# A two-layer attention and ConvFFN trunk on one Trainium2 core: near-attention operands and results through DRAM scratch, earlier sums of h, and two more gate pairs a layer as seven-product blocks

## The chip, the core and the metric

The kernel runs on one core of one Trainium2 chip. The metric is the device time of one execution in microseconds (us). The kernel before takes 2670.75 us, the median of three runs (2669.71 to 2671.51). The engines are TensorE (PE; its weight loads have a row of their own, PEld), VectorE (DVE), ScalarE (ACT) and GpSimd (POOL). SyncE (SP) issues nearly all DMAs. Each engine takes its instructions in order.

## The reference

Sequence length and model width are 1024, there are 2 layers, all data are fp32. One layer computes:

```
h = rmsnorm(x, norm1)
qa, ka, va, qb, kb, vb, gate_pre = split(h @ w_in)
o_a = dilated_mixture(qa, ka, va)        # 12 heads of 64: 3 groups of 4 heads,
                                         # (window, dilation) = (128, 1), (512, 4), (2048, 16)
o_b = stick_breaking_attention(qb, kb, vb)             # 4 heads
g_a, g_b = split(sigmoid(gate_pre + b_gate))           # 1024 columns each
x = x + (g_a * (o_a @ w_br[:256]) + g_b * (o_b @ w_br[256:])) @ w_o
up = rmsnorm(x, norm2) @ w_up            # 2816 columns of a, 2816 of v
x = x + (gelu(causal_conv(a)) * v) @ w_down
```

In `dilated_mixture` each query sees 128 earlier keys at its group's step; the three groups' results are mixed by their softmax denominators. Group 0 (dilation 1) is the undilated branch, called near below; groups 1 and 2 are far. Stick-breaking attention is causal, with a cumulative product along the keys.

## The kernel before

**Numbers in two parts.** Every matmul operand is split into a high part `hi` (rounded, by ACT) and a rest `lo` (by DVE, `split`, L135 and L140). A product is three matmuls: hi by hi, hi by lo, lo by hi. The tokens are two halves `n` of 512, the width 8 chunks of 128; `H[n]` holds h in its two parts.

**Plain product** (`product`, L171 to L173): one unit of 128 columns of `w_in` against both halves takes 2 x 8 x 3 = 48 matmuls of 512 columns. `gate` (L1145, tile `g_ps`), `keys`, `queries` use it.

**Pair in seven products** (`pair`, `seven`, L935 to L937, tiles `i_a`, `i_b`, `i_c`): two units of 128 columns against both halves are a 2 x 2 block product done with seven block products instead of eight: 7 x 4 x 3 = 84 matmuls. For this it needs four sums of blocks of h: S1 = b12 - b11, S2 = b22 - S1, S3 = b22 - b12, S4 = b21 - S2 (`block_sums`, tile `h_sum`), where b11, b12, b21, b22 are halves of `H[1]`, `H[0]` in their first and last four chunks. S1 to S3 take two buffers each of the six of tag `e8`; S4 is written over b12 and thus needs every plain product done.

**The attentions and their filler.** `attend` walks through the items by hand: 16 stick-breaking items (B00 to B17), then near items (N), then 16 far items (T). An item is scores on PE, then softmax or scan work on DVE and ACT, then for each set of key blocks `turn` (transposes on PE, split by ACT and DVE) and `apply` (matmuls with V). After each such slot `dense.advance(rate)` adds `rate` steps of dense work; a step is 6 matmuls of 512 columns (12 of 256 for `values`). `RATE_B` has the rates of the B items, `RATE[1]` that of N, `RATE[2:]` those of T. The class `Dense` takes units from `main`, then `plain` (gates, `PLAIN` of them), then `seven` (the remaining gates as pairs). Units of `main` marked True are pairs and start once `plain` is empty. `dense.side` holds the steps of the sums, one popped at each `advance`.

**Near operands.** `keys` and `queries` keep k and q of one pair of heads in `e8` tiles `kt`, `qt` and in `ql` (tag `ql`, two buffers); per half four or two 64-row ACT copies and two 64-row DVE operations. A near item is one head (N00 to N11), with four scores and five turns, at rate 0.85. Results go to tile `on` (tag `xa`, four buffers) and for stick-breaking to `ob` (one `e8` buffer), which goes to DRAM once.

**Far operands.** `pair_kq` and `pair_v` store to DRAM (`tk`, `tv`) and each far item loads its own; item T00 may start when both v pairs, the first two kq pairs and near item N11 are done, plus `LEAD` = 6 steps. The other two kq pairs and the four gate pairs run beside the far items or after them (`finish`).

**FFN.** The first two of 22 units run in plain products while `norm` for the second half is still being made (L492 to L495), the others in seven products (`up`); `up` has a POOL subtraction at L1514. The buffers of tag `pt` (six) hold most short-lived 128 x 512 tiles.

PE's order is the program's. On the other engines and on SP the scheduler orders by priority; `tc.high_priority` moves instructions ahead.

Of the kernel before, what the change touches and what calls it, by code (L numbers as in the profile page):

```python
# [16 lines left out]
P = 128  # L17
# [25 lines left out]
RATE = (0.68, 0.85, 0.72, 0.62)  # L43
RATE_B = (0.9, 1.6, 0.75, 1.1, 0.65, 0.9, 0.6, 0.3)
PLAIN = 8
# [12 lines left out]
def trunk_kernel(ctx, tc, x, norm1, w_in, b_gate, w_br, w_o, norm2, w_up, conv_w, conv_b, w_down, norm_f, out, depth=None, probe=None):  # L58
# [58 lines left out]
    dn = [dr.tile([4, T], F32, name=f"dn{i}") for i in range(2)]  # L117

# [92 lines left out]
    class Dense:  # L211
# [4 lines left out]
        def __init__(self):  # L216
            self.main, self.plain, self.seven, self.done = [], [], [], set()
            self.side, self.later, self.hooks = [], {}, []
            self.now = self.nxt = None
            self.due, self.count = 0.0, 0  # L220
            self.started = False
            self.scored = self.applied = self.kq = self.v = 0
# [46 lines left out]
        def step(self):  # L269
            while True:  # L270
                if self.now is None:
# [4 lines left out]
                    if self.now[2] and not self.started:  # L276
# [4 lines left out]
                        self.started = True  # L281
                if self.nxt is None:
# [44 lines left out]
    def attend(dense, items):  # L327
# [4 lines left out]
        for i, (name, first, rest, rate, make) in enumerate(items):  # L332
# [37 lines left out]
            for j, f in enumerate(seq):  # L370
                if nxt and j >= at:
# [100 lines left out]
    def norm(n, gain, tag, then=None, keep=False):  # L472
# [17 lines left out]
        for e in range(KD):  # L490
            hf = kept_f32(n, e) if keep else small("hf")
            dve.scalar_tensor_tensor(hf, xc(n, e), gain[:, e : e + 1], rb, ALU.mult, ALU.mult)  # L492
            hi, lo = H[n][0][:, e, :], H[n][1][:, e, :]
            act.copy(hi, hf)
            (pool if e % 2 and not (keep and n) else dve).tensor_tensor(lo, hf, f32(hi), ALU.subtract)  # L495
# [80 lines left out]

    def head(l):
# [51 lines left out]
    def stick_item(pr, s, qp):  # L629
        if "ob" not in R:  # L630
            R["ob"] = big("ob")
        q, k, vt, ob = R["qb", pr], R["kb", pr], R["vb"], R["ob"]
# [52 lines left out]
        def apply(kb):  # L685
# [24 lines left out]
    def near_item(pr, s):  # L710
        if s == 0:
            R["st0", pr] = sb.tile([P, 2, 2, 8], F32, tag="st0", bufs=2, name="st0")
        if "on" not in R:
            R["on"] = sb.tile([P, 2, T], F32, tag="xa", bufs=4, name="on")
        q, k, vt, on, st = R["q0", pr], R["k0", pr], R["v0"], R["on"], R["st0", pr]
        slot = 2 * pr + s
        got, shared = {}, {}

        def score(m):
            if m == 0:  # L720
                shared["bias"] = sb.tile([P, 512], F32, tag="bias", name="bias0")
                dve.tensor_scalar(shared["bias"][:, 0:256], base0, SLOPES[slot], None, ALU.mult)
            if m % 2 == 0:
                got[m // 2] = sb.tile([P, T], F32, tag="p4", bufs=4, name="p0")
            z = bank("s", "z0")
            todo = []
            for j in range(2):
# [3 lines left out]
                scores(zz, *(t[:, s, b * P : b * P + P] for t in q), k[:, s, (b - 1) * P + c : b * P + P])  # L731
                todo.append((b, c, zz))
            for b, c, zz in todo:
                pp = got[b // 4][:, 256 * (b % 4) + c : 256 * (b % 4) + 256]
                nm = st[:, 0, s, b : b + 1]
                dve.tensor_tensor_reduce(pp, zz, shared["bias"][:, c:256], 1.0, 3e38, ALU.add, ALU.min, nm)
                act.activation(pp, pp, AF.Exp, bias=nm, scale=-1.0, accum_out=st[:, 1, s, b : b + 1])

        def turn(i, some):
            tp = bank("t", "t0")  # L740
            w = 0
            for kb, bs in some:
                for b in bs:
                    col = 256 * (b % 4) + (P if b == kb else 0)
                    pe.transpose(tp[:, w * P : (w + 1) * P], got[b // 4][:, col : col + P], ident)
                    w += 1
            shared[i] = parts(tp, w * P, "p0")

        def apply(i, some, n, first, last):
# [4 lines left out]
            for kb, bs in some:  # L754
                c0, nb = (bs[0] - 4 * n) * P, len(bs) * P
                for p in (0, 1):
# [3 lines left out]
                        shared[i][p][:, w * P : w * P + nb],  # L760
# [5 lines left out]
            if last:  # L766
                fold(on[64 * s : 64 * s + 64, pr, n * HF : (n + 1) * HF], o)
# [8 lines left out]
        micro = []  # L776
        for n, sets in enumerate(
            (
                [[(0, [0, 1]), (1, [1, 2])], [(2, [2, 3]), (3, [3])]],
                [[(3, [4]), (4, [4, 5])], [(5, [5, 6]), (6, [6, 7])], [(7, [7])]],  # L780
            )
        ):
            for i, some in enumerate(sets):
                micro.append(
                    (
                        lambda i=(n, i), some=some: turn(i, some),
                        lambda i=(n, i), some=some, n=n, f=(i == 0), la=(i == len(sets) - 1): apply(i, some, n, f, la),
                    )
                )
        return [lambda m=m: score(m) for m in range(4)], micro  # L790


# [14 lines left out]
    def far_item(dense, pr, s, r, share):  # L807
        i = 8 * pr + 4 * s + r
        slot = 2 * pr + s
        if s == 0 and r == 0:  # L810
            R["st1", pr] = sb.tile([P, 2, 2, 2, 4], F32, tag="st1", bufs=2, name="st1")
            R["ot", pr] = None
        st = R["st1", pr]
# [127 lines left out]
    def block_sums():  # L941
# [4 lines left out]
        def first(t, a, b, i):  # L946
            if i == 0:
                if "r" not in keep:
                    keep["r"] = quarter("h_sum")
                new_s(t)  # L950
            r, (ah, al), (bh, bl) = keep["r"][:, i, :], a()[i], b()[i]
            one = pool.tensor_tensor(r, f32(al), f32(bl), ALU.subtract)
            if "last" in keep:
                tc.add_manual_dep(one.ins, keep["last"], NO_SYNC, reason="one sum after the other")
            pool.tensor_tensor(r, r, f32(ah), ALU.add)
# [1063 lines left out]
```

## Time and profile before

| | |
|---|---|
| median of 3 runs | 2670.75 us |
| profiled execution, its own time | 2670.63 us |
| span in that profile | 2668.9 us |
| ACT busy | 1350.2 us (51%) |
| instructions | 36664 |

The profile gives busy time by engine, by stage (a window of the span) and by group of instructions. A matmul's duration is the time it is in the array, and several are in it at once: matmuls of 512 columns that last 389 ns each start much closer together than that. So the sum of their durations is more than the time they take, and a busy PE may still be held up by a fraction between starts. The rate has to be read from counts over a window, or from starts in the timeline.

### The profile page before, as it was taken

To read this page: it belongs to the slowest core of one execution; us is meant where nothing else is said; L and a number is where in the kernel's file an instruction comes from. 1 tells how busy PE (TensorE), PEld (TensorE's weight loads), DVE (VectorE), ACT (ScalarE), POOL (GpSimd) and SP (SyncE) were. 2 spreads that over 40 slices of the span, in tenths; PEclk is the share of its full clock that TensorE was granted. 3 is DMA by queue.
4 is the path that set the end of the run, shared out by engine and by line. 5 is a ranking of instruction groups with operands and counts; after the bars stand their busy time and mean duration, and the time that the engine had idled before them with its cause. 6 is when DMAs were issued, how large, how long until landed. Compare 5 with 4: busy or idle time off the path is not lost.

```text
span 2668.9 us, 36664 instructions
## 1 busy us (share of the span) xinstructions
PE 2651.1 (99%) x13084; PEld 2227.4 (83%) x13084; DVE 2030.3 (76%) x3087; ACT 1350.2 (51%) x2490; POOL 648.9 (24%) x473
## 2 busy tenths in 40 slices
PE   9999999999999999999999999999999999999999
PEld 8988888878888888888889888888888888888888
DVE  5877856685888888897658777566858888898865
ACT  6556645564545554432445565455645454554225
POOL 2003210121233443321210051110321343343200
PEclk9999999999999999999999999999999999999999
DMA  5212178573244544688411122885632544446863
GB/s 183 64 52 83 58 206 242 187 260 99 80 145 139 174 139 158 228 313 321 152 40 40 51 81 84 220 246 182 233 94 68 180 144 149 151 166 246 339 243 118
DMA packets 360194, 424.19 MB, mean 159 GB/s; under 512 B 20692, under 2 KB 289356, under 8 KB 357964
## 3 DMA queue, kind: packets, MB, share of 16 engines
q1 hardware_dynamic: 359996, 421.85, 47.6%
q8 instruction: 103, 1.69, 0.3%
q14 instruction: 79, 0.65, 0.1%
q10 hardware_dynamic: 16, 0.00, 0.0%
HBM read 278.07 MB, written 143.72 MB: 158 GB/s over the span
## 4 chain that ended last, share of the span: by engine, by line
PE 90%; DVE 7%; issue 1%; ACT 1%; DMA 1%; POOL 0%; DVEq 0%; ACTq 0%; SPq 0%; POOLq 0%
PE u_a L935 5%; PE u_a L936 5%; PE u_a L937 5%; PE d_ps L1647 5%; PE d_ps L1648 5%; PE d_ps L1649 5%; PE u_c L935 3%; PE u_c L936 3%; PE u_c L937 3%; PE i_a L935 3%; PE i_a L936 2%; PE i_a L937 2%; PE o_ps L171 2%; PE o_ps L173 2%; PE o_ps L172 2%; PE g_ps L171 2%
## 5 line engine op out<-in xcount | busy, mean ns | idle before, releaser
L140 DVE TENSOR_TENSOR w_lo<-up_a,w_hi 128x512 fp32r<-128x512 f32 x240 | 236.8, 993 | 20.3 <-ACT w_hi L135 20.3
L135 ACT CAST w_hi<-up_a 128x512 fp32r<-128x512 f32 x240 | 149.4, 623 | 183.9 <-PE u_a L936 45.8
L1655 DVE TENSOR_TENSOR x<-x,d_ps 128x512 f32<-128x512 f32 (+1 forms) x228 | 152.0, 672 | 77.9 <-PE d_ps L1649 76.4
L1386 POOL TENSOR_TENSOR cv<-cv 128x512 f32<-128x512 f32 x88 | 131.8, 1508 | 249.3 <-DVE cv L1381 139.4
L140 DVE TENSOR_TENSOR g<-cv,g 128x512 fp32r<-128x512 f32 x154 | 151.2, 983 | 5.2 <-ACT g L135 2.8
L140 DVE TENSOR_TENSOR w_lo<-w_raw,w_hi 128x512 fp32r<-128x512 f32 x144 | 109.4, 762 | 52.8 <-ACT w_hi L135 52.6
L135 ACT CAST w_hi<-w_raw 128x512 fp32r<-128x512 f32 x144 | 89.5, 621 | 111.1 <-PE o_ps L172 64.3
L140 DVE TENSOR_TENSOR w_lo<-in_a,w_hi 128x512 fp32r<-128x512 f32 x120 | 88.9, 740 | 60.4 <-ACT w_hi L135 54.7
L135 ACT CAST w_hi<-in_a 128x512 fp32r<-128x512 f32 x120 | 74.6, 622 | 118.3 <-PE i_c L936 51.3
L1647 PE MATMUL d_ps<-gd_in,w_hi 128*128 128x512 f32 (+1 forms) x340 | 130.3, 383 | 1.6 <-issue 0.7
L1649 PE MATMUL d_ps<-gd_in,w_lo 128*128 128x512 f32 (+1 forms) x340 | 129.8, 382 | 0.0
L1648 PE MATMUL d_ps<-gd_in,w_hi 128*128 128x512 f32 (+1 forms) x340 | 129.8, 382 | 0.0
L935 PE MATMUL u_a<-hh,w_hi 128*128 128x512 f32 x320 | 124.7, 390 | 0.5 <-DVE u L1537 0.5
L937 PE MATMUL u_a<-hh,w_lo 128*128 128x512 f32 x320 | 124.5, 389 | 0.0
L935 PE MATMUL u_a<-t_hi,w_hi 128*128 128x512 f32 x320 | 124.5, 389 | 0.0
L936 PE MATMUL u_a<-hl,w_hi 128*128 128x512 f32 x320 | 124.5, 389 | 0.0
L936 PE MATMUL u_a<-t_lo,w_hi 128*128 128x512 f32 x320 | 124.5, 389 | 0.0
L937 PE MATMUL u_a<-t_hi,w_lo 128*128 128x512 f32 x320 | 124.5, 389 | 0.0
L135 ACT CAST g<-cv 128x512 fp32r<-128x512 f32 x154 | 94.9, 616 | 42.2 <-POOL cv L1386 29.5
L665 DVE TENSOR_TENSOR_SCAN stay<-stay,zero 128x512 f32<-128x512 f32 (+2 forms) x96 | 93.5, 974 | 28.0 <-ACT stay L651 27.4
L1647 PE MATMUL d_ps<-gd_in,wd 128*128 128x512 f32 (+1 forms) x292 | 113.9, 390 | 0.0
L1649 PE MATMUL d_ps<-gd_in,wd 128*128 128x512 f32 (+1 forms) x292 | 112.8, 386 | 0.0
(412 smaller groups left out, 8603.5 us busy)
## 6 DMA issues: line engine op xcount, KB each, us to landing
gd<-g SPq DMA_DIRECT2D x154, 512.0 KB, 3.5
gd_in<-gd SPq DMA_DIRECT2D x154, 512.0 KB, 6.0
up_a<-in_w_up_dram SPq DMA_DIRECT2D x80, 512.0 KB, 5.3
t_kq<-tk SPq DMA_DIRECT2D x32, 768.0 KB, 4.4
wd_raw<-in_w_down_dram SPq DMA_DIRECT2D x22, 1024.0 KB, 12.1
w_raw<-in_w_in_dram SPq DMA_DIRECT2D x80, 256.0 KB, 3.0
in_a<-in_w_in_dram SPq DMA_DIRECT2D x40, 512.0 KB, 3.9
gin<-gs SPq DMA_DIRECT2D x32, 512.0 KB, 4.4
```

The costliest lines, as they stand in the source:

```text
L135: one = act.copy(hi, src)
L140: two = dve.tensor_tensor(lo, src, f32(hi), ALU.subtract)
L171: pe.matmul(o, lh, rh, start=(first and i == 0), stop=False, skip_group_check=share)
L665: one = dve.tensor_tensor_scan(rev, rev, zero[:, 0:1].to_broadcast([P, c1 - c0]), 1.0 if c1 == L else sv[:, c1 : c1 + 1], ALU.mult, ALU.add)
L935: pe.matmul(o, w[0][:, c], rh, start=(first and i == 0), stop=False, skip_group_check=True)
L936: pe.matmul(o, w[0][:, c], rl, start=False, stop=False, skip_group_check=True)
L937: pe.matmul(o, w[1][:, c], rh, start=False, stop=(last and i == 3), skip_group_check=True)
L1386: return lambda: pool.tensor_tensor(dst, a, b, ALU.subtract)
L1647: pe.matmul(o[:, sub], wh[:, c], gh[:, sub], start=(i == 0 and k in (0, 4, 5)), stop=False, skip_group_check=True)
L1648: pe.matmul(o[:, sub], wh[:, c], gl[:, sub], start=False, stop=False, skip_group_check=True)
L1649: pe.matmul(o[:, sub], wl[:, c], gh[:, sub], start=False, stop=(i == m - 1), skip_group_check=True)
L1655: dve.tensor_tensor(x, x, o[:, sub], ALU.add)
```

## The change

- `PLAIN` 8 to 4: four gate units a layer leave the plain products, and two more gate pairs are done in seven products.
- Near k and q: `near_kq` makes the product, splits it over 128 rows with one ACT and one DVE instruction a half, and stores the parts to DRAM (`nk`). Each near item (now half a head, N0 to N7) loads its operands with two DMAs into a buffer of tag `xa`; the load is issued two items ahead, and the item may start 6 steps after (8 for the first, which also waits for the last B item).
- Results: `ob` and `on` pieces are folded into `pt` tiles and stored at once; `on` is loaded back when the far items begin. The `e8` buffer of `ob` is gone.
- Sums: S3 starts when B07 is scored, S1 and S2 when B17 is; S2 = S3 + b11. POOL does 33 of the 48 additions a layer (24 of 40 before), DVE 15. S4 is made in the first six steps of the first pair. Far pairs may start after B17 and beside the near items, no longer after the last near score.
- Rates: B items 0.9 of before; near 0.85 to 1.0; far 0.72 and 0.62 to 0.9 and 0.75. T00 waits 10 steps after its loads, no longer 6.
- FFN: for the second half the last chunk of h has high priority; in `up` the subtraction L1514 goes to DVE for the third unit alone.

```diff
-RATE = (0.68, 0.85, 0.72, 0.62)
-RATE_B = (0.9, 1.6, 0.75, 1.1, 0.65, 0.9, 0.6, 0.3)
-PLAIN = 8
+RATE = (0.68, 1.0, 0.9, 0.75)
+RATE_B = (0.81, 1.44, 0.675, 0.99, 0.585, 0.81, 0.54, 0.27)
+PLAIN = 4
+SUMS = ((1, 0, 0, 0, 0, 6), (1, 1, 0, 1, 2, 8), (1, 2, 0, 2, 4, 10), (1, 3, 0, 0, 7, 12), (2, 0, 1, 3, 9, 11), (2, 1, 0, 1, 9, 14), (2, 2, 1, 3, 11, 13), (2, 3, 1, 3, 13, 15))
...
-                return i < 16 and {"N11", f"1{i // 8}", f"2{i // 8}", "v1", "v2"} <= self.done
+                return i < 16 and {"N7", f"1{i // 8}", f"2{i // 8}", "v1", "v2"} <= self.done
+            while self.near < min(8, self.nscored + 2) and {"B17", f"0{self.near // 4}"} <= self.done:
+                fetch_near(self.near)
+                self.at(LEAD if self.near else 8, lambda i=self.near: self.done.add(f"G{i}"))
+                self.near += 1
...
-                self.at(LEAD, lambda i=self.kq: self.done.add(f"F{i}"))
+                self.at(LEAD if self.kq else 10, lambda i=self.kq: self.done.add(f"F{i}"))
...
+                        for k, f in enumerate(self.first):
+                            self.at(1 + k, f)
...
+            with tc.high_priority(offset=AHEAD) if keep and n and e >= 7 else nullcontext():
...
+    def near_kq(pr, l, off, query):
+        w = weights(w_in[l][:, off : off + P], P)
+        yield
+        for n in range(2):
+            o = bank("ps", "q_ps" if query else "k_ps")
+            yield from product(o, [(w[k], h_part(n, k)) for k in range(KD)])
+            hi, lo = small("nk_h", F32R), small("nk_l", F32R)
+            if query:
+                act.mul(hi, o, -SCALE)
+                dve.scalar_tensor_tensor(lo, o, -SCALE, f32(hi), ALU.mult, ALU.subtract)
+            else:
+                act.copy(hi, o)
+                dve.tensor_tensor(lo, o, f32(hi), ALU.subtract)
+            for s in range(2):
+                rows = slice(64 * s, 64 * s + 64)
+                for src, kind, up in ((hi, 1, 0), (hi, 1, 64), (lo, 2, 0)) if query else ((hi, 0, 0), (lo, 0, 64)):
+                    nc.sync.dma_start(nk[pr][s, up : up + 64, kind, n * HF : (n + 1) * HF], f32(src[rows]))
+            yield
...
-                fold(ob[64 * s : 64 * s + 64, pr, qp * 256 : (qp + 1) * 256], o)
-                if (pr, s, qp) == (1, 1, 3):
-                    nc.sync.dma_start(obd, ob)
+                part = small("ob_p")[64 * s : 64 * s + 64, 0:256]
+                fold(part, o)
+                nc.sync.dma_start(obd[64 * s : 64 * s + 64, pr, qp * 256 : (qp + 1) * 256], part)
...
+    def fetch_near(i):
+        pr, s, n = i // 4, i // 2 % 2, i % 2
+        t = R["nk", i] = sb.tile([P, 2048], F32R, tag="xa", bufs=4, name="n_kq")
+        k0 = 3 * P * n
+        nc.sync.dma_start(f32(t[:, 0 : (n + 1) * HF - k0]), nk[pr][s, :, 0, k0 : (n + 1) * HF])
+        nc.sync.dma_start(f32(t[:, 640:1664]).rearrange("p (a c) -> p a c", a=2), nk[pr][s, :, 1:3, n * HF : (n + 1) * HF])
...
-                fold(on[64 * s : 64 * s + 64, pr, n * HF : (n + 1) * HF], o)
+                part = small("on_p")[64 * s : 64 * s + 64]
+                fold(part, o)
+                nc.sync.dma_start(ond[64 * s : 64 * s + 64, pr, n * HF : (n + 1) * HF], part)
...
+            less = ALU.add if t == 2 else ALU.subtract
+            one = eng.tensor_tensor(r, f32(al), f32(bl), less)
+            eng.tensor_tensor(r, r, f32(ah), ALU.add)
+            one = eng.tensor_tensor(r, r, f32(bh), less)
...
-        series({"B17"}, 3, lambda i: first(3, b22, b12, i), 6, 4)
-        series({"N01s"}, 1, lambda i: first(1, b12, b11, i), 6, 4)
-        for i in range(4):
-            todo.append(({"N01s"}, lambda i=i: less(b22, i)))
-        series({"N11s"}, 2, lambda i: i or new_s(2), 0, 1)
-        series({"plain"}, 4, lambda i: further(4, b21, i), 1, 1)
+        todo += series("B07s", *((3, i, pool, i % 2, 4 * i, 4 * i + 6) for i in range(4)))
+        todo += series("B17s", *((t, i, (pool, dve)[e], slot, at, then) for t, i, e, slot, at, then in SUMS))
+        dense.first = [f for _, f in series("", *((4, i, (pool, dve)[e], slot, at, then) for i, e, slot, at, then in ((0, 0, 0, 0, 4), (1, 1, 3, 0, 2), (2, 0, 1, 2, 6), (3, 1, 3, 3, 5))))]
...
-            *kq("0", 0, {"B07s"}, 0, -SCALE),
-            *kq("0", 1, {"B17s"}, P, -SCALE),
-            (None, {"N11s"}, pair_v(dense, l, 1), True),
+            *kq("0", 0, set(), 0, -SCALE),
+            *kq("0", 1, set(), P, -SCALE),
+            (None, {"B17"}, pair_v(dense, l, 1), True),
...
-            pool.tensor_tensor(a11, a12, a11, ALU.subtract)
+            (dve if j == 2 else pool).tensor_tensor(a11, a12, a11, ALU.subtract)
```

More of the change, by code (lines that the diff above doesn't have):

```diff
@@ L370, in attend @@
             for j, f in enumerate(seq):
+                if pending and name[0] == "N":
+                    begin()
+                    at = max(at, j)
                 if nxt and j >= at:
@@ L491, in norm @@
             hf = kept_f32(n, e) if keep else small("hf")
[L492 to L495, printed above, removed]
+            with tc.high_priority(offset=AHEAD) if keep and n and e >= 7 else nullcontext():
+                dve.scalar_tensor_tensor(hf, xc(n, e), gain[:, e : e + 1], rb, ALU.mult, ALU.mult)
+                hi, lo = H[n][0][:, e, :], H[n][1][:, e, :]
+                act.copy(hi, hf)
+                (pool if e % 2 and not (keep and n) else dve).tensor_tensor(lo, hf, f32(hi), ALU.subtract)
             if e < KD - 1:
@@ L969, in in_two @@
         def in_two(t, i):
-            split(*S[t][i], keep["r"][:, i, :], "waits")
+            split(*S[t][i], keep.pop((t, i)), "waits")
         b11, b12, b21, b22 = (lambda n=n, k=k: half(n, k) for k in range(2) for n in (1, 0))
         todo = []
-        def series(after, t, f, lag, gap):
-            at = {}
-            for i in range(4):
-                at.setdefault(i * gap, []).append(lambda i=i: f(i))
-                at.setdefault(i * gap + lag, []).append(lambda i=i: in_two(t, i))
-            for k in range(3 * gap + lag + 1):
-                todo.append((after, lambda fs=at.get(k, ()): [g() for g in fs]))
@@ L1185, in mixer @@
         dense.seven = [pair_gate(dense, l, e) for e in range(PLAIN // 2, KD)]
-        dense.side = [({"B02"}, zeros)] * (l == 0) + block_sums()
+        dense.side = [({"B02"}, zeros)] * (l == 0) + block_sums(dense)
         def kq(name, pr, after, off, scale):
-            offk, offq = (OFF_KB, OFF_QB) if name == "b" else (OFF_KA, OFF_QA)
+            if name == "0":
+                return [(None, after, near_kq(pr, l, OFF_KA + off, False), False), ("0" + str(pr), after, near_kq(pr, l, OFF_QA + off, True), False)]
+            offk, offq = OFF_KB, OFF_QB
             return [
```

133 lines of the change are left out of this document (72 added, 61 removed).

## The prediction

> **What bounds the kernel now.** I read the page first: engine shares and granted clock.
>
> ```profile
> span 2668.9 us, 36664 instructions
> ...
> PE 2651.1 (99%) x13084; PEld 2227.4 (83%) x13084; DVE 2030.3 (76%) x3087; ACT 1350.2 (51%) x2490; POOL 648.9 (24%) x473
> ...
> PEclk9999999999999999999999999999999999999999
> ```
>
> PE is never idle and its clock never drops, so time goes only where matmuls go, if the busy figure can be trusted. To see how many a busy PE does, I took stages of layer 0 (PE, PEld, DVE, ACT, POOL busy, instructions in brackets): stick-breaking items, near items, four pairs alone, far items, branch products, FFN opening, steady FFN.
>
> ```profile
> 67.00:247.00 180.00, 179.73 (x1058) 157.14 (x1057) 140.40 (x250) 108.29 (x235) 10.94 (x10) 1.00 0.21 59
> 247.00:325.00 78.00, 78.00 (x426) 66.24 (x425) 58.83 (x122) 49.95 (x118) 31.64 (x23) 1.00 0.24 75
> 325.00:410.00 85.00, 84.97 (x391) 69.81 (x390) 49.54 (x75) 36.50 (x64) 10.98 (x8) 1.00 0.70 193
> 410.00:547.00 137.00, 135.61 (x761) 115.31 (x760) 92.27 (x199) 74.39 (x166) 16.36 (x15) 1.00 0.69 215
> 547.00:600.00 53.00, 51.13 (x239) 41.48 (x237) 48.27 (x67) 35.74 (x60) 15.86 (x12) 1.00 0.79 271
> 700.00:760.00 60.00, 59.08 (x263) 48.20 (x263) 53.81 (x87) 32.56 (x55) 9.88 (x8) 1.00 0.28 91
> 760.00:1300.00 540.00, 539.26 (x2376) 445.67 (x2376) 455.75 (x554) 237.92 (x376) 178.93 (x120) 1.00 0.58 206
> ```
>
> In the steady FFN 540 us hold 2376 matmuls: 227 ns each. The timeline there shows the same, beside a duration of 0.39:
>
> ```profile
> 1000.21 0.39 PE L936 MATMUL u_c<-hl,w_hi 128*128 128x512 f32 x1
> 1000.43 0.39 PE L937 MATMUL u_c<-hh,w_lo 128*128 128x512 f32 x1
> 1000.66 0.39 PE L935 MATMUL u_c<-hh,w_hi 128*128 128x512 f32 x1
> ```
>
> So a 512-column matmul is worth **227 ns, not the 390 of its row**, and a step of dense filler (6 of them) 1.36 us. PE's waits that show at all are small and scattered:
>
> ```profile
> PE o L858 <- DVE p1l L140: 2.1, 6, 0.7
> PE br_ps L171 <- DVE gin L1301: 2.0, 4, 0.8
> ...
> PE z L608 <- DVE st L840: 1.5, 3, 0.6
> PE u_ps L172 <- DVE hl L495: 1.3, 2, 0.7
> ```
>
> Each is PE behind DVE. The kernel is bound by matmul count; the next limit is DVE, above all where a stage needs it for 85% or more.
>
> **Part 1, the gates: fewer matmuls.**
>
> ```profile
> L171 PE MATMUL g_ps<-hh,w_hi 128*128 128x512 f32 x256 | 105.6, 412 | 0.0
> L935 PE MATMUL i_b<-hh,w_hi 128*128 128x512 f32 x80 | 33.0, 412 | 0.0
> ```
>
> The 256 are one of three lines of 16 plain gates: 48 matmuls a gate. The 80 are four of the 12 matmuls of one product in each of 20 pairs: 84 a pair. A layer loses four gates (192) and gains two pairs (168): 24 fewer, 48 in both layers. 48 x 0.227 = **-10.9 us**. From the durations (390) it would be -18.7; I take the count, since starts and not ends decide when the next one goes. No other edit adds or removes a PE instruction: the near items keep their scores, transposes and applies, only cut in two.
>
> **Part 2, near operands and results through scratch.** Per layer eight halves of k or q are split on 128 rows instead of 64: ACT goes from 24 operations to 8, DVE from 16 to 8.
>
> ```profile
> L548 ACT ACTIVATE qt<-q_ps 64x512 fp32r<-64x512 f32 x32 | 19.0, 593 | 20.3 <-PE q_ps L173 20.0
> ...
> L559 POOL MEMSET ql<- 64x1024 f32 x16 | 15.2, 949 | 355.2 <-PE z L609 253.4 <-issue 83.0 <-PE nrm_t L478 10.1
> ```
>
> That spares ACT some 9 us a layer and POOL four memsets (3.8 us), all off the path. SP gets 40 stores of k and q, 16 loads, 15 more stores of `ob`, 8 of `on` and one load: 80 more per layer, and four once for zeros. The nearest rows, by issue time (min, median, max) and by KB and landing:
>
> ```profile
> L1146 SPq DMA_DIRECT2D gs<-gt x32: 319/338/343, 132.8 to 1635.7; - x32
> L1092 SPq DMA_DIRECT2D tk<-kq_h x96: 574/614/1538, 352.3 to 1773.0; - x96
> ...
> t_kq<-tk SPq DMA_DIRECT2D x32, 768.0 KB, 4.4
> ...
> tk<-kq_h SPq DMA_DIRECT2D x96, 128.0 KB, 2.5
> ```
>
> 80 x 0.34 to 0.61 is 27 to 49 us of SP over the 533 us from 67 to 600. Queued behind a store that waits for its split are the loads of gate and pair weights, whose users are more than one unit (8 steps, 11 us) away. The near loads land in about 4.4 us against a lead of 6 steps, 8.2 us; only if SP holds them for 3.8 us or more do they show, since then `until` puts dense work in the gap and PE does not stop. The load of `on` has eight far items before its first use, and the four steps more before T00 are pair steps that have to be done anyway: nothing for both. Cost of the scratch between 0 and, if `pt` buffers are held by stores (2.5 us) when ACT wants one, the longest wait above (0.8) at each of 16 splits: 13 us. I take **+0.5 us a layer**, by the far operands, which are stored in this way from the same buffers and show no PE wait of their own.
>
> **Part 3, sums and pairs into the near stage.** Near slots stay 56 (turns, applies, scores); filler goes from 0.85 x 56 = 47.6 steps to 56, so the stage grows from 78 to 78 + 8.4 x 1.36 = 89.5 us, time that is taken out elsewhere. Of the plain steps, 128 before, 96 are left; the B items take 85 x 0.9 = 76.5 and ten run alone before N0, so some 46 of the 56 are pair steps. What DVE then needs:
>
> ```profile
> L140 DVE TENSOR_TENSOR t_lo<-h_sum,t_hi 128x512 fp32r<-128x512 f32 x12 | 9.4, 798 | 0.1
> ...
> L966 DVE TENSOR_TENSOR h_sum<-hh,h_sum 128x512 f32<-128x512 f32 x8 | 6.4, 804 | 0.0
> L967 DVE TENSOR_TENSOR h_sum<-h_sum,hl 128x512 f32<-128x512 f32 x7 | 5.8, 824 | 0.1
> L140 DVE TENSOR_TENSOR w_lo<-w_raw,w_hi 128x512 fp32r<-128x512 f32 x6 | 5.6, 941 | 2.1 <-ACT w_hi L135 2.0
> L140 DVE TENSOR_TENSOR p0l<-t,p0h 128x512 fp32r<-128x512 f32 x7 | 4.8, 689 | 3.8 <-ACT p0h L135 3.8
> ...
> L140 DVE TENSOR_TENSOR p0l<-t,p0h 128x384 fp32r<-128x384 f32 x8 | 4.4, 551 | 2.6 <-ACT p0h L135 2.5
> ```
>
> From 58.8: out go the old sums (-12.2), the splits of S3 (-3.2), most gate splits (-4.6), the last near k and q (-5.6), the first pair's start, which was already in (-3); in come 15 additions at 0.8 (+12) and 46 pair steps at the price of the stage of pairs alone, 49.5 us for 391/6 = 65 steps, 0.76 (+35). Sum 77, **86% of 89.5**. The steady FFN runs at 455.75/540 = 84% with PE idle 0.74 us; the branch stage at 48.27/53 = 91% idles 1.87 us. Between these, nearer the FFN: **+1.5 us a layer** (bounds 0 and 1.87 x 89.5/53 = 3.2).
>
> The B items lose 8.5 steps (11.6 us) and gain S3's splits: DVE 140/168 = 83%, with 10% less filler per slot. Work that hides their scans is thinner; bounds 0 and 3, within the 0.5 of part 2. The far items get 66 steps instead of 53.6 over 80 slots, so p1l and st come earlier relative to PE: of 1.39 us idle I take off **0.5 a layer** (bounds 0 and 1.39).
>
> [...]
>
> **Part 4, FFN opening.**
>
> ```profile
> 717.79 0.39 PE L173 MATMUL u_ps<-hh,w_lo 128*128 128x512 f32 x1
> ...
> 718.30 0.50 PE L171 MATMUL u_ps<-hh,w_hi 128*128 128x512 f32 x1
> ...
> 719.45 0.50 PE L172 MATMUL u_ps<-hl,w_hi 128*128 128x512 f32 x1 [0.65 <-DVE hl L495]
> ```
>
> Against 0.227 these starts are late by 0.28 and 0.92: 1.2 us, because the last chunk's hh and hl stand behind sums on DVE. With priority they go first; the sums behind them (S1, S2, needed by the third unit) are late next, and the third unit's subtraction joins DVE. Bounds -1.2 and +1 (the same wait moved on); **-0.7 a layer**.
>
> **Sum**: 2668.9 - 10.9 + 2 x (0.5 + 1.5 - 0.5 - 0.7) = 2659.6 of span; the execution had 1.7 beside its span (2670.63), and its time is 0.1 under the median. **2661 us.**
>
> **Rivals.**
> 1. *The gain is eaten by buffers and SP in the B stage* (part 2's upper bound): 16 splits at 0.35 to 0.8 us plus thinner filler take back 6 to 13 us; 2666 to 2672, say 2669. For: B stages have 83% DVE and the chain score, scan, transpose. Against: `ob` frees an `e8` buffer, so two `stay` tiles can stand side by side.
> 2. *DVE becomes the bound of the near stage; slower.* If all of the pairs' operations beside POOL cost what the FFN's splits do, 993 ns against a median of 691 now,
>
> ```profile
> L140 DVE TENSOR_TENSOR w_lo<-up_a,w_hi 128x512 fp32r<-128x512 f32 x240 | 236.8, 993 | 20.3 <-ACT w_hi L135 20.3
> ...
> L140 DVE TENSOR_TENSOR w_lo<-in_a,w_hi x120: 675/691/1706, 297.7 to 1868.7; 128x512 fp32r<-128x512 f32 x120
> ```
>
> the 35 us grow by three quarters of 44%, to 47, the need to 88; at the FFN's 84% that takes 105 us, 15 more than planned, twice: 2661 - 3 + 30 = 2688. It is slower from a need of (89.5 + 9) x 0.844 = 83 us on, where 2658 + 18 passes 2676. For: turns wait on DVE only one or two slots after their scores. Against: POOL does little more there than before, 31.6 us in 78.
> 3. *More gain*: priorities and denser filler also remove most idle time of the far, branch and opening stages (1.39 + 1.87 + 0.92 a layer), and the near stage costs nothing: 2670.7 - 10.9 - 7 = 2653. Against: the branch stage isn't touched.
> 4. *It doesn't do what it says*: near loads are late so often that items start behind dense work alone, and the far stage then lacks filler; the idle 1.39 us of the far stage would have to become ten, 2670. Counted with rival 1.
>
> **How the numbers follow.** Forecast (2656 to 2665) 0.52; rival 3 0.14; rivals 1 and 4 0.18; rival 2 0.16. A measurement of this kernel tells 0.2% (5.3 us) from no change, so the forecast and rival 3 are faster, 0.66; rivals 1 and 4 the same, 0.18; rival 2 slower, 0.16. Range **2652 to 2678**: it holds the forecast, rivals 1 and 4, two thirds of rival 3 and the near half of rival 2.
>
> **What would show it.** Matmuls 13036 instead of 13084, g_ps lines 128 each, i_b 96. Part 3 is right if a window of the near items has DVE at 83 to 90% and PE idle under 2 us. Part 4 is right if L495 no longer stands among PE's waits. PE waits on p0l, on `nk` stores or in the B stage of more than 5 us in all would make the prediction wrong, as would less than 45 us of dense work beside the near items.

## The result and the profile after

The change made the kernel slower, by 1%. Its median is 2698.95 us (2697.37 to 2699.47, four runs) beside 2671.13 us (2669.71 to 2673.18, four runs) for the kernel before in the same comparison: a ratio of 1.0102, 95% interval 1.009 to 1.0114, or 28 us. The prediction was 2661, its range ended at 2678.

The page's first lines for the kernel after:

```profile
span 2695.6 us, 37001 instructions
...
PE 2649.3 (98%) x13036; PEld 2225.5 (83%) x13036; DVE 2079.2 (77%) x3103; ACT 1335.7 (50%) x2470; POOL 685.2 (25%) x489
...
PEclk9999999999999999999999999999999999999999
```

The 48 matmuls are gone, as computed. PE's busy time is almost what it was, the clock row shows nothing, and yet the span is 26.7 us longer. PE's waits (total us, times, longest):

```profile
PE sb_o L724 <- DVE sbl L143: 16.1, 10, 4.6
PE sb_t L712 <- DVE beta L700: 9.1, 8, 1.9
PE u_c L976 <- ACT u L1573: 3.2, 2, 1.6
PE z L641 <- DVE st L778: 2.2, 2, 1.3
...
PE u_a L978 <- DVE w_lo L143: 1.5, 2, 0.8
```

The first two rows are new in size: 25.2 us in the two layers, all in the stick-breaking items, all PE behind DVE. The kernel before has no row for `sb_o`, and this one for `sb_t`:

```profile
PE sb_t L681 <- DVE beta L669: 0.5, 2, 0.2
```

The stages say the same. To compare stages whose filler differs, I use the **stall**: each gap between the starts of two successive matmuls, less the median gap behind a matmul of the same width in the kernel before, summed over a stage (layer 0 / layer 1, us). It holds waits, and also what a lower clock costs.

| stage | before: time, stall | after: time, stall |
|---|---|---|
| first `sb_t` to last `sb_o` (stick-breaking) | 174.6 / 174.6, 2.3 / 2.3 | 172.1 / 171.2, 18.9 / 18.0 |
| to the first far score | 165.6 / 165.6, 1.8 / 1.7 | 150.2 / 150.1, 5.4 / 5.3 |
| to the first branch product | 151.6 / 151.0, 6.2 / 5.5 | 181.5 / 182.5, 3.4 / 4.4 |
| branch products | stall 2.1 / 1.1 | stall 2.0 / -0.1 |
| first 70 us of the FFN | stall 1.9 / 2.1 | stall 3.1 / 3.1 |

For layer 0: -5.5 (24 matmuls at 0.227) + 16.6 + 3.6 - 2.8 - 0.1 + 1.2 = +13.0 us; for layer 1: -5.5 + 15.7 + 3.6 - 1.1 - 1.2 + 1.0 = +12.5. Together 25.5 of the span's 26.7. **The stick-breaking stage alone loses more than the whole net.** Its window, before and after (us, then busy time of PE, PEld, DVE, ACT, POOL with instructions, granted clock, DMA share, GB/s):

```profile
70.80:245.40 174.60, 174.33 (x1031) 152.62 (x1029) 136.75 (x240) 105.84 (x227) 9.42 (x9) 1.00 0.19 57
```

```profile
71.70:243.70 172.00, 159.22 (x934) 138.03 (x933) 150.58 (x226) 95.69 (x201) 41.97 (x27) 0.99 0.38 99
```

The stage holds 97 fewer matmul records, yet is only 2.6 us shorter. DVE issues fewer instructions than before and is busy 14 us longer: 150.58 us, where the stage without its stall would last 172.0 - 18.9 = 153.1, so DVE would need 98% of it. POOL has 42 us where it had 9.4. Groups of DVE in the window from 67 to 247 us (line, operation, output and inputs, count, busy us, mean ns, idle before), before:

```profile
L140 DVE TENSOR_TENSOR sbl<-sb_t,sbh 128x512 fp32r<-128x512 f32 x24 | 16.4, 685 | 6.4 <-ACT sbh L135 6.4
...
L665 DVE TENSOR_TENSOR_SCAN stay<-stay,zero 128x256 f32<-128x256 f32 x8 | 5.7, 717 | 1.2 <-ACT stay L651 1.1
...
L665 DVE TENSOR_TENSOR_SCAN stay<-stay,zero 128x128 f32<-128x128 f32 x8 | 3.6, 453 | 1.6 <-ACT stay L651 1.5
...
L669 DVE TENSOR_TENSOR beta<-beta,stay 128x127 f32<-128x127 f32 x8 | 2.3, 290 | 0.2
```

and after:

```profile
L143 DVE TENSOR_TENSOR sbl<-sb_t,sbh 128x512 fp32r<-128x512 f32 x24 | 16.3, 681 | 4.6 <-ACT sbh L138 3.9 <-DMA nk<-nk_h 0.7
...
L696 DVE TENSOR_TENSOR_SCAN stay<-stay,zero 128x256 f32<-128x256 f32 x8 | 6.9, 860 | 0.8 <-ACT stay L682 0.7
...
L143 DVE TENSOR_TENSOR t_lo<-h_sum,t_hi 128x512 fp32r<-128x512 f32 x7 | 6.1, 878 | 0.0
...
L696 DVE TENSOR_TENSOR_SCAN stay<-stay,zero 128x128 f32<-128x128 f32 x8 | 5.0, 628 | 0.6 <-ACT stay L682 0.5
...
L1007 DVE TENSOR_TENSOR h_s<-t_lo,hl 128x512 f32<-128x512 f32 x3 | 4.3, 1423 | 0.0
L700 DVE TENSOR_TENSOR beta<-beta,stay 128x127 f32<-128x127 f32 x8 | 4.2, 525 | 0.2
```

The same scans and products, with the same shapes, are longer; `sbl`, which reads PSUM, is not (681 ns, 685 before). Over all nine groups of scans and `beta` products, DVE has 10.2 us more than before. The sums it does itself (seven additions in this window) add 8.6, and the nine `t_lo` splits 8.5.

The longest wait, in the timeline (start, us, engine, line, operation; in brackets the idle time and what ended it):

```profile
238.72 1.74 DVE L143 TENSOR_TENSOR t_lo<-h_s,t_hi 128x512 fp32r<-128x512 f32 x1
240.38 1.74 DVE L1011 TENSOR_TENSOR h_s<-h_s,hh 128x512 f32<-128x512 f32 x1
242.05 0.68 DVE L1007 TENSOR_TENSOR h_s<-t_lo,hl 128x512 f32<-128x512 f32 x1
242.65 0.55 DVE L143 TENSOR_TENSOR sbl<-sb_t,sbh 128x384 fp32r<-128x384 f32 x1
```

```profile
238.32 1.59 POOL L1010 TENSOR_TENSOR h_sum<-h_sum,t_hi 128x512 f32<-128x512 f32 x1
239.99 1.59 POOL L1011 TENSOR_TENSOR h_sum<-h_sum,hh 128x512 f32<-128x512 f32 x1
```

```profile
243.25 0.58 PE L724 MATMUL sb_o<-sbl,vb 128*128 128x256 f32 x1 [4.56 <-DVE sbl L143]
```

DVE's two instructions at 238.72 and 240.38 take 1.74 us and end at 240.46 and 242.12, each some 0.55 us after the POOL instruction beside it (239.91, 241.58). The third, of the same kind, starts after POOL has stopped: 0.68. So most of what such an instruction takes without POOL fell behind POOL's end. `sbl`, whose ACT half `sbh` ends at 238.26, stands behind them, and PE behind `sbl`: its next filler matmul, on `g_ps`, starts at 243.96.

The sums also run far from their place. The program puts S1 and S2 behind the scores of B17, the last stick-breaking item, which PE makes from 218 us on. POOL's first sums run at 88 us, and those of S1 from 156 us:

```profile
88.19 1.32 POOL L1007 TENSOR_TENSOR h_sum<-hl 128x512 f32<-128x512 f32 x1 [21.70 <-DVE z L680]
...
156.47 1.69 POOL L1007 TENSOR_TENSOR h_sum<-hl,hl 128x512 f32<-128x512 f32 x1 [0.63 <-DVE t_lo L143]
...
232.13 1.32 POOL L1007 TENSOR_TENSOR h_sum<-hl,hl 128x512 f32<-128x512 f32 x1 [61.27 <-DVE t_lo L143]
```

h is there long before. From S3's third part on, a sum on POOL waits only for the split `t_lo` that frees its buffer slot, or for the sum ahead of it; the wait of the very first is put down to a DVE instruction on `z`. In the kernel before, the buffer itself was late:

```profile
239.54 1.30 POOL L952 TENSOR_TENSOR h_sum<-hl 128x512 f32<-128x512 f32 x1 [15.06 <-PE sb_o L693]
```

There the sums began 6 us before the last stick-breaking product (245.4 us).

### The profile page after: what moved, and what is told of

It reads as the page before. It is cut to its first block, busy times and chain, and to the rows that moved or that the text cites. A ratio compares the mean times of both kernels' runs of the same rounds, so it can differ in the third digit from the quotient of the medians.

```text
span 2695.6 us, 37001 instructions
## 1 busy us (share of the span) xinstructions
PE 2649.3 (98%) x13036; PEld 2225.5 (83%) x13036; DVE 2079.2 (77%) x3103; ACT 1335.7 (50%) x2470; POOL 685.2 (25%) x489
## 4 chain that ended last, share of the span: by engine, by line
PE 83%; DVE 10%; DMA 2%; ACT 2%; issue 2%; POOL 1%; SPq 0%; DVEq 0%; ACTq 0%; POOLq 0%
PE u_a L978 5%; PE u_a L977 5%; PE u_a L976 5%; PE d_ps L1696 4%; PE d_ps L1698 4%; PE d_ps L1697 4%; PE i_a L976 3%; PE i_a L978 3%; PE i_a L977 3%; PE u_c L976 3%; PE u_c L977 3%; PE u_c L978 3%; PE o_ps L174 2%; PE o_ps L175 2%; PE o_ps L176 2%
## 5 line engine op out<-in xcount | busy, mean ns | idle before, releaser
L143 DVE TENSOR_TENSOR w_lo<-in_a,w_hi 128x512 fp32r<-128x512 f32 x144 | 107.0, 743 | 74.8 <-ACT w_hi L138 74.6
L138 ACT CAST w_hi<-in_a 128x512 fp32r<-128x512 f32 x144 | 89.1, 619 | 136.3 <-PE i_a L977 52.8
L1069 POOL TENSOR_TENSOR u<-in_a 128x512 f32<-128x512 f32 x24 | 32.9, 1375 | 456.1 <-PE v_t L1150 107.0
L143 DVE TENSOR_TENSOR w_lo<-w_raw,w_hi 128x512 fp32r<-128x512 f32 x128 | 97.2, 765 | 47.0 <-ACT w_hi L138 46.5
L138 ACT CAST w_hi<-w_raw 128x512 fp32r<-128x512 f32 x128 | 79.4, 621 | 102.7 <-PE o_ps L175 60.7
L696 DVE TENSOR_TENSOR_SCAN stay<-stay,zero 128x512 f32<-128x512 f32 (+2 forms) x96 | 101.6, 1059 | 20.2 <-ACT stay L682 19.5
L1696 PE MATMUL d_ps<-gd_in,wd 128*128 128x512 f32 (+1 forms) x292 | 114.0, 391 | 0.0
```

The source lines that it names most:

```text
L138: one = act.copy(hi, src)
L143: two = dve.tensor_tensor(lo, src, f32(hi), ALU.subtract)
L696: one = dve.tensor_tensor_scan(rev, rev, zero[:, 0:1].to_broadcast([P, c1 - c0]), 1.0 if c1 == L else sv[:, c1 : c1 + 1], ALU.mult, ALU.add)
L1696: pe.matmul(o[:, sub], wh[:, c], gh[:, sub], start=(i == 0 and k in (0, 4, 5)), stop=False, skip_group_check=True)
```

## The experiments

Each is an edit of the kernel after, timed beside the kernel before. The diffs show the lines that matter; `...` stands for what is left out, and an edit that an earlier experiment showed is named and not shown again. The theory was that the sums, moved into the stick-breaking stage, overload DVE there; its forms differ in how (POOL slowing DVE, too early, too dense, first in DVE's order). The rivals were the lower rate of filler, the scratch transfers, and the FFN's opening.

| edit | median us | before us | ratio, 95% interval | stick-breaking stall |
|---|---|---|---|---|
| none | 2698.95 | 2671.13 | 1.0102, 1.009 to 1.0114 | 18.9 / 18.0 |
| all sums on DVE | 2679.82 | 2671.03 | 1.0033, 1.002 to 1.0047 | 11.8 / 10.5 |
| POOL's sums held at their place | 2708.83 | 2671.03 | 1.0141, 1.0126 to 1.0157 | 23.7 / 23.5 |
| old rates of the items | 2693.92 | 2671.03 | 1.0088, 1.0071 to 1.0105 | 16.7 / 17.1 |
| no sums | 2668.1 | 2671.03 | 0.9988, 0.9979 to 0.9998 | 5.6 / 6.1 |
| S3 on DVE | 2695.46 | 2671.04 | 1.0092, 1.0076 to 1.0108 | 17.1 / 16.1 |
| S1, S2 on DVE | 2693.32 | 2671.04 | 1.0086, 1.0072 to 1.01 | 16.2 / 15.6 |
| sums on DVE, old rates, old FFN | 2677.09 | 2671.04 | 1.0024, 1.0013 to 1.0034 | 10.8 / 10.8 |
| sums on DVE, after the last B item | 2705.0 | 2671.04 | 1.0129, 1.0115 to 1.0144 | 5.7 / 6.4 |
| sums on DVE, spread, old FFN | 2681.99 | 2671.99 | 1.0037, 1.0025 to 1.005 | 11.7 / 13.0 |
| no sums, old rates, old FFN | 2665.04 | 2671.99 | 0.9974, 0.9964 to 0.9984 | 6.5 / 4.9 |
| FFN subtraction back on POOL | 2701.01 | 2671.99 | 1.0111, 1.0095 to 1.0126 | 18.8 / 18.0 |
| sums on DVE, item work first, old FFN | 2683.83 | 2671.99 | 1.0042, 1.003 to 1.0055 | 13.6 / 12.7 |

**All sums on DVE.** POOL then does none of the 33 additions.

```diff
+            eng = dve
             r = keep[t, i] = place(slot)
```

> All 48 additions of the sums a layer on DVE, none on POOL. Theory A (POOL's sums hold up DVE's operations in the stick-breaking stage, which then hold up PE): DVE has 33 more additions of about 0.69 us a layer, 23 us, but nothing is stretched (scans of 128 columns back from 1.45 to 0.45 us), most PE waits of the stick-breaking stage go: 2675 to 2690 us. Theory B (10% less filler a slot): as the changed kernel or slower, 2697 or more. Theory C (what counts is DVE's own load, whichever engine disturbs it): slower than the changed kernel, 2705 or more.

19 us of the 28 come back. The stick-breaking window:

```profile
71.60:236.50 164.90, 157.66 (x934) 136.81 (x933) 148.22 (x251) 95.83 (x201) 0.00 (x0) 1.00 0.40 104
```

and one of the groups of DVE (window 67 to 240 us):

```profile
L700 DVE TENSOR_TENSOR beta<-beta,stay 128x127 f32<-128x127 f32 x8 | 2.3, 286 | 0.2
```

`beta` is back at 286 ns, from 525, with POOL at zero. That POOL stretched DVE is shown. The other number is as telling: DVE, with 25 instructions more, is busy 148.22 us instead of 150.58. Doing the additions on POOL had spared DVE nothing.

**POOL's sums held at their place in the program.** A small ACT copy, placed behind the ACT half of the items' latest split, must come first.

```diff
+            if eng is pool:
+                here = act.copy(r[:, 0:1], eps)
+                tc.add_manual_dep(here.ins, LAST["act"], NO_SYNC, reason="in turn")
             one = eng.tensor_tensor(r, f32(al), f32(bl), less)
```

> Each POOL sum waits for a one-column ACT write in its own buffer that stands at the sum's place in the program, so that POOL no longer runs ahead of it (18 ACT writes a layer more). Theory A, in the form that POOL runs its sums too early: S3's sums no longer fall at 88 us and S1's no longer at 156 us but after B07 and B17 are scored; the waits at 93 us go, those at 150 to 173 shrink, the long one at 238 us stays: 2685 to 2693. Theory B: no change within 3 us, 2696 to 2702. Theory C: no change, 2696 to 2702.

It is 10 us slower still, not faster, and slower than any of the forms had it. POOL's first sum of S3 now starts at 131.68 us and that of S1 at 219.45; its last of S2 ends at 246.02, still inside the stage. So running early was not the fault in itself: held back, the same sums meet items that are just as loaded, closer together. (The copies themselves add little: ACT has 1.4 us more in the stage.) Window and wait:

```profile
71.40:248.20 176.80, 161.40 (x935) 139.51 (x933) 154.04 (x227) 97.05 (x210) 44.90 (x27) 0.98 0.37 97
```

```profile
PE sb_o L724 <- DVE sbl L143: 22.9, 13, 4.2
```

**The old rates of the items.**

```diff
-RATE_B = (0.81, 1.44, 0.675, 0.99, 0.585, 0.81, 0.54, 0.27)
+RATE_B = (0.9, 1.6, 0.75, 1.1, 0.65, 0.9, 0.6, 0.3)
```

> RATE_B as in the kernel before (10% more filler beside the stick-breaking items), all else as changed. Theory B: the stick-breaking stage's lost time goes, 2660 to 2672. Theory A: PE has 8.5 steps more to put into waits of 1 to 5 us, some of which it covers: 2688 to 2697. Theory C: as A.

5 us of 28: more filler covers some waits, but the stall stays at 16.7 / 17.1. The thinner filler is not the main cause.

**No sums.** S1 to S4 are replaced by halves of h that exist already, so the additions and their splits are left out, and the pairs multiply by those halves in place of the sums.

```diff
-        todo += series("B07s", ...)
-        todo += series("B17s", ...)
-        dense.first = [...]
+        S[1], S[2], S[3], S[4] = b12(), b22(), b21(), half(0, 0)
+        dense.first = []
```

> The four sums of h are left out (the pairs use unsummed blocks, so the outputs are other than the reference's); all matmuls stay. Theories A and C: the stick-breaking stage runs as before the change, 2650 to 2662. Theory B: 20 us a layer stay lost there, 2685 or more.

30.9 us less than after, though not the 2650 to 2662 that was expected. The window:

```profile
71.80:230.50 158.70, 156.31 (x934) 136.50 (x933) 128.82 (x215) 90.63 (x191) 0.66 (x1) 1.00 0.41 107
```

The stage keeps its scratch stores and loads (DMA share 0.41) and its filler (934 matmul records, as after) and loses 13 us. So neither the scratch nor the rates hold much. A stall of 5.6 us remains, against 2.3 before.

**S3 alone, or S1 and S2 alone, on DVE.**

```diff
+            eng = dve if t == 3 else eng
```

> Only S3's 12 additions a layer move from POOL to DVE; S1, one of S2 and two of S4 stay on POOL. With all of them moved the kernel gained 19 us (2679.8). Theory A1 (S3 in the middle of the stick-breaking items is what costs): most of the 19, 2682 to 2688. Theory A2 (the sums at its end, when the long scans of B16 and B17 run, are what costs): 2690 to 2697.

```diff
+            eng = dve if t in (1, 2) else eng
```

> The mirror of the run before: S1 and S2 wholly on DVE, S3 on POOL. A1: 2690 to 2697. A2: 2682 to 2688, the PE wait of 4.6 us at 238 us and its half clock gone.

They gain 3.5 and 5.6 us; all sums together, S4's too, gained 19. Each run came out in the range that laid the cost to the other's sums, so no one sum is the culprit, and the gains do not add. It is not that the additions moved to DVE are stretched by those left on POOL: in the first run S3's have means of 668 to 685 ns, in the second all groups of S1 and S2 but one (1040 ns) have 679 to 691, as with all sums on DVE (674 to 691). Why the gains don't add stays open.

**All sums on DVE, the rates and both FFN edits undone.** The fastest version with all of the computation.

```diff
-RATE_B = (0.81, 1.44, 0.675, 0.99, 0.585, 0.81, 0.54, 0.27)
+RATE_B = (0.9, 1.6, 0.75, 1.1, 0.65, 0.9, 0.6, 0.3)
...
-            with tc.high_priority(offset=AHEAD) if keep and n and e >= 7 else nullcontext():
+            with tc.high_priority(offset=AHEAD) if False else nullcontext():
...
+            eng = dve
...
-            (dve if j == 2 else pool).tensor_tensor(a11, a12, a11, ALU.subtract)
+            pool.tensor_tensor(a11, a12, a11, ALU.subtract)
```

> All additions on DVE, RATE_B as before, and FFN's opening as before. If the three add up: 2679.8 - 5 (rates, from the run with them alone) - 2.5 (FFN's opening, whose waits are 1.2 us a layer longer after the change) = 2672, no different from the kernel before. If the rates only hid POOL's waits: 2677.

2.7 us less than with the sums' engine alone, and the FFN's stall is back at 1.9 / 2.2, which is 2.1 us of it in two layers. The rates are then worth nothing that can be told. It does not reach the kernel before.

**All sums on DVE, after the last stick-breaking item**, each held behind the items' latest DVE split.

```diff
+            eng = dve
...
+            tc.add_manual_dep(one.ins, LAST["dve"], NO_SYNC, reason="in turn")
...
-        todo += series("B07s", ...)
-        todo += series("B17s", ...)
+        late = [(t, i, dve, i % 2, 8 * n + 2 * i, 8 * n + 2 * i + 1) for n, t in enumerate((3, 1, 2)) for i in range(4)]
+        todo += series("B17", *late)
```

> All additions on DVE, and none before the last stick-breaking item is done: S3, S1, S2 in the some 30 us in which dense work runs alone and the first near items begin. If the stick-breaking stage's waits are those of the sums, its 11 us of waits a layer fall to the 6 of the run without sums, and the near stage, which then has 36 additions and 12 splits (33 us of DVE) more, decides: 2665 to 2672 if they fit, 2680 or more if the first pair waits for its sums.

The stick-breaking stage then behaves as without sums, and the stretch behind it pays more. The two windows, and two of PE's waits:

```profile
71.80:230.70 158.90, 156.31 (x933) 136.49 (x932) 129.44 (x214) 90.56 (x192) 1.36 (x2) 1.00 0.41 107
...
230.70:300.00 69.30, 55.93 (x252) 45.65 (x251) 62.78 (x123) 33.69 (x77) 4.83 (x3) 0.85 0.30 95
```

```profile
PE z L641 <- DVE st L778: 10.8, 2, 5.4
PE t L787 <- ACT p L779: 8.9, 2, 4.4
```

DVE has 62.78 of 69.3 us, PE stands for up to 5.4 us at a time, and the granted clock averages 0.85. From the last B item to the first far score the stall is 22.4 / 21.8.

**All sums on DVE, evenly spread** over the items (12 slots from one of the four parts of S3 to the next, 3 for S1 and S2), each held behind the items' latest DVE split, old FFN.

```diff
-        todo += series("B07s", ...)
-        todo += series("B17s", ...)
+        todo += series("B07s", *((3, i, dve, i % 2, 12 * i, 12 * i + 2) for i in range(4)))
+        todo += series("B17s", *((t, i, dve, i % 2, 12 * n + 3 * i, 12 * n + 3 * i + 1) for n, t in enumerate((1, 2)) for i in range(4)))
```

> All additions on DVE, one sum at a time and further apart: S3 over the second pair's stick-breaking items (12 slots a sum), S1 and S2 from B17's score on (3 slots a sum), each held behind the split last issued; FFN's opening as before. If waits come from sums standing in a row on DVE, the stick-breaking stage's stall falls from 11 us to 7 and the near stage stays at 4: 2668 to 2673. If DVE's mere load counts, as the run with all sums on DVE less FFN's 2.4: 2677.

Stall 11.7 / 13.0, against 11.8 / 10.5 without the spreading: the spacing doesn't help. The time is above both that were expected, and the attempt to beat the kernel before failed.

**No sums, old rates, old FFN**: with the sums left out again, what is left of the change is the gates, the scratch and the near and far order.

> As the run without sums (they are left out, the outputs are other than the reference's), with RATE_B and FFN's opening as before: what is left is the gate swap and the scratch. If the thinner filler is what held its stick-breaking stage at 5.6 us of stall against 2.3 before: 2668.1 - 2.4 (FFN) - 6 = 2660, the full 10.9 us of the matmul count. If the scratch stores hold it up: 2665 or more.

7 us faster than before, of the 10.9 that the gates give. Of the missing 4, part can be seen at one place of each layer, where the first pair's POOL work meets a `beta` product. In layer 0:

```profile
232.24 1.36 POOL L1068 TENSOR_TENSOR u<-in_a 128x512 f32<-128x512 f32 x1 [8.98 <-DMA in_a<-in_w_in_dram]
...
232.59 1.57 DVE L700 TENSOR_TENSOR beta<-beta,stay 128x511 f32<-128x511 f32 x1
```

```profile
PE sb_t L712 <- DVE beta L700: 4.1, 2, 2.1
```

In layer 1 `beta` takes 1.57 us from 1548.71, beside a POOL instruction that ends at 1549.73, and PE waits 2.06. So the pairs, started sooner, bring POOL work into the stage as well. These two waits alone are as long as what is missing; how they, the scratch and gains elsewhere add up was not separated.

**The FFN's subtraction back on POOL**, the priority kept.

```diff
-            (dve if j == 2 else pool).tensor_tensor(a11, a12, a11, ALU.subtract)
+            pool.tensor_tensor(a11, a12, a11, ALU.subtract)
```

> The change with the subtraction of the third FFN unit back on POOL; the priority of the last chunk of h stays. If the move to DVE is what makes FFN's opening longer (waits of 1.7 us on u_c and 0.9 us on u_a a layer), these waits go and 2.4 us or more are gained: 2694 to 2697. If it is the priority, they stay: 2698 to 2700.

The times with and without can't be told apart (the intervals overlap), and this one lies just above what either reading expected; the waits can:

```profile
PE u_c L976 <- ACT u L1573: 4.6, 2, 2.3
```

4.6 us in two layers, 3.2 with the subtraction on DVE. The subtraction on DVE gives back 0.7 a layer, so it is the priority that costs: with it alone the first 70 us stall for 3.8 / 3.8, with neither edit (sums on DVE, old rates) for 1.9 / 2.2.

**Item work first on DVE.** All sums on DVE, old FFN, and the scans, `beta` products and near score operations at high priority.

```diff
-                with tc.high_priority(offset=AHEAD) if soon else nullcontext():
+                with tc.high_priority(offset=AHEAD):
...
+                with tc.high_priority(offset=AHEAD):
                     dve.tensor_tensor_reduce(pp, zz, share["bias"][:, c:256], 1.0, 3e38, ALU.add, ALU.min, nm)
                     act.activation(pp, pp, AF.Exp, bias=nm, scale=-1.0, accum_out=st[:, 1, s, b : b + 1])
```

> All additions on DVE at the change's places, FFN's opening as before, and the scans and near scores on DVE ahead of the sums by priority. If PE waits because sums stand ahead of the operations that PE needs: stall of the stick-breaking stage from 11 to 7 us a layer or less, 2666 to 2672. If DVE is simply short of time there: 2677.

Not better: 13.6 / 12.7, and slower than both times that were expected. The priority hardly changed the order: from 140 to 170 us DVE runs the same sums in front of the same scans as with the sums on DVE alone, but for a few neighbours that changed places. So whether another order would help was not tested. That DVE is short of time is the reading that the runs leave. The window has DVE at 147.84 of 166.80 us:

```profile
71.60:238.40 166.80, 158.59 (x935) 137.03 (x933) 147.84 (x251) 95.95 (x201) 0.00 (x0) 0.99 0.39 103
```

## Why the prediction was wrong

**Part 1, the gates: right in count; 7 of its 10.9 us could be shown.** 13036 matmuls, and these groups of PE (line, operation, count, busy us, mean ns):

```profile
L174 PE MATMUL g_ps<-hh,w_hi 128*128 128x512 f32 x128 | 54.2, 423 | 0.0
...
L976 PE MATMUL i_b<-hh,w_hi 128*128 128x512 f32 x96 | 39.4, 410 | 0.0
```

The run without sums, rates and FFN edits showed 7 of the 10.9 us.

**The step that failed is the DVE need of the stick-breaking stage**, in part 3's second paragraph: "The B items lose 8.5 steps (11.6 us) and gain S3's splits: DVE 140/168 = 83%", with bounds 0 and 3, within part 2's 0.5. The stage took +16.6 and +15.7 us of stall a layer. Three things in that sentence were wrong:

1. It put S1 and S2 into the wrong stage. I counted them for the near items, but the place that the program gives them, behind B17's scores, is itself in the stick-breaking stage: held there, POOL ran them from 219.45 to 246.02 us, in a stage that ends at 248.2. Unheld they ran earlier still, since a sum has no late operand; only its buffer held it, and the change gives it a free one. All sums but S4 were done before the first near score (261.57 us), with 27 POOL instructions in the stage.
2. It priced only what DVE itself executes. I had rows in which DVE is longer beside POOL's sums (part 3's `t_lo` with 798 ns, while `p0l`, which reads PSUM, has 689) and put that into the near stage as rival 2, while the stage whose DVE work is scans and products of two SBUF tiles was counted without it. Of the additions, DVE's own seven take 8.6 us, the scans and products beside POOL 10.2 more: together 18.8, and the 32 additions that the run with all sums on DVE does from 67 to 240 us cost it 21.7 us. Some 42 us of POOL saved almost nothing.
3. 83% was set against the stage as it would be with filler to cover every wait. The stage had 88% (150.58 of 172.0), and 98% of its unstalled length. The runs with the new rates order themselves roughly by this: DVE busy 128.82 and 129.44 us go with a stall of 5.6 and 5.7, 147.84 and 148.22 with 13.6 and 11.8, 149.28 (S1 and S2 on DVE) with 16.2, 150.58 with 18.9, 151.43 (S3 on DVE) with 17.1, 154.04 with 23.7. Part of that busy time is stretch, so this goes with the cause and doesn't prove it; the runs that take the sums out of the stage do.

**Rival 2 had the cost beside POOL and not the place**; its chance was 0.16 and its price 2688, my estimate from two rows (993 and 691 ns). The near items, for which I wrote a DVE share of 83 to 90%, have much less, since the sums were over by then:

```profile
261.50:350.00 88.50, 87.53 (x477) 74.18 (x476) 62.90 (x150) 55.94 (x138) 6.47 (x5) 1.00 0.61 171
```

71%, and PE idle for 0.97 us. So the near stage's term (+1.5) had the wrong cause; between the last B item and the first far score the stall did grow by 3.6, mostly by a granted clock of 0.50, which the last section shows. Rival 1 had the place (the stick-breaking stage) but laid it to buffers and SP: the run without sums has all of the scratch traffic and loses 13 us of stall in layer 0.

**Part 2, the scratch**: +0.5 a layer is neither confirmed nor refuted; with the sums out and rates and FFN undone, 4 us in both layers are missing, and two waits behind `beta` beside the pairs' POOL work are as long as that.

**Part 3's far items**: -0.5 a layer was the right sign; -2.8 and -1.1 were measured.

**Part 4, the FFN's opening: the sign was wrong.** The wait on `hl` is gone from PE's list, as predicted, but the next two waits of the list shown above (`u_c` and `u_a`, 3.2 and 1.5 us) took its place: +1.2 and +1.0 a layer instead of -0.7. That is just beyond the upper bound, "the same wait moved on".

The test that was named beforehand, more than 5 us of waits in the B stage, is what the profile showed: 25.2.

## What to carry to other kernels

Moving work to an engine "with time to spare" had a price on its neighbour here, 10.2 us of DVE's scans and products: before counting an addition on POOL as free for DVE, look at whether DVE's operations in that stage have two SBUF inputs (here `beta` with two went from 290 to 525 ns, `sbl` with one from 685 to 681), and take the stretch from a row where both already run together. A moved operation can run when its last operand or buffer comes free, not where the program names it (S1's sums at 156 us for a place at 218), so look for what held it before and whether the change takes that away. A stage with DVE at 78% hid its waits with filler; 14 us more of DVE used up that cover, and putting the filler back gave only 5 us.

## What the runs showed of the hardware

**POOL's additions cost DVE as much as doing them on DVE.** In the stick-breaking stage 42 us of POOL went with 150.58 us of DVE, none with 148.22. A scan of 128 columns went from a mean of 453 to 628 ns, `beta` of 127 columns from 290 to 525. The narrow operations grew most here: the scans of 512 columns only from 1230 to 1278, the products from 690 to 747. All of these have two SBUF inputs; `sbl` with its one SBUF input stayed at 681 ns (685 before). The two instructions of 1.74 us in front of the longest wait end some 0.55 us after POOL's; without POOL beside it, one of that kind took 0.68.

**Three waits were paid for again in the clock.** Windows of the kernel after, around two of them:

```profile
150.40:153.80 3.40, 1.17 (x8) 0.87 (x7) 3.40 (x4) 2.91 (x7) 3.32 (x3) 1.00 0.00 0
153.80:157.20 3.40, 3.21 (x9) 2.73 (x10) 3.40 (x5) 0.00 (x0) 2.69 (x3) 0.51 0.33 77
238.60:242.60 4.00, 0.10 (x1) 0.00 (x0) 4.00 (x4) 0.44 (x1) 2.90 (x2) 1.00 0.27 102
242.60:249.40 6.80, 6.14 (x16) 4.99 (x17) 6.74 (x10) 2.09 (x5) 4.10 (x3) 0.50 0.44 135
```

Behind the wait that ends at 243.25 (4.56 us) the granted clock stays at 0.50 until 249.4, and matmuls of 512 columns start 0.43 us apart (244.49, 244.92) instead of 0.227: by the clock's share some 3.1 us of work lost, most of it after the stick-breaking stage has ended (243.7): 2.8 of the 3.6 us by which the stall of the stage behind it grew in layer 0. Behind the wait that ends at 154.0 (0.96 us) it is 0.51 until 157.2, another 1.6 us. In the window ahead of it PE was busy for 1.17 of 3.40 us, with 1.46 as its longest single wait, so here the clock fell though PE had not stood all the time; ahead of the fall at 242.6 it was busy for 0.10 of 4.00. In layer 1 the clock is 0.50 from 1573.8 to 1580.6, around the end of the long wait at 1575.2 (4.55 us): 2.7 us. Together that is 7.4 us of work, beside the 25.2 us of waits; no run takes the clock alone away.
